# V and the gates of an mLSTM layer: from a plain product to seven products of 520-column quarters

## The chip, the cores and the metric

One core of a Trainium2 chip runs one program. Its time is device microseconds (us); the kernel before has a median of 2306.89 us over three runs (2303.06 to 2307.14). Five engines work side by side: TensorE (PE in the profile, with its weight loads apart as PEld), VectorE (DVE), ScalarE (ACT), GpSimd (POOL) and SyncE (SP), whose queue issues nearly all transfers. Each engine takes its instructions in the order in which they were written into its queue, and an instruction that waits holds up all behind it on that engine.

## The reference

A trunk of two layers over 2048 and 256 tokens of width 1024, in f32. The second layer is a bidirectional mLSTM:

```
xn = rms_norm(x, norm_g[1])
proj = xn @ w_in            # 1024 x (512 q + 512 k + 1024 v + 1024 o + 1024 z + 16 gates)
g = (g + gate_bias).reshape(B, S, 4, MLSTM_HEADS)   # input and forget gate, forward and backward
h = mlstm_chunkwise(q, k, v, ig_f, fg_f) + flipped(mlstm_chunkwise on the flipped sequence)
y = x + (norm(h) * sigmoid(o) * silu(z)) @ w_out
```

The change touches the columns v and g of `proj`: 1024 + 16 = 1040 columns for each token.

## The kernel before, in words

The 2304 tokens are 18 tiles of 128 (`NT`), worked on in nine pairs (`PAIRS`). The program runs in stages: attention (`attn_core`), then products of all tokens with a weight matrix: z (`attn_gate`), the attention's output (`attn_out`), q and k, and V with the gates (both in `mlstm_qkv`), z and o of the mLSTM in two passes (`mlstm_gates_states`), and at last `mlstm_core`. In this text the two passes of `mlstm_gates_states` are called oz0 and oz1.

To come near f32 with a faster number format, every operand is split into a high and a low part (`split` for tokens, `part` for weights: ScalarE makes the high part, VectorE the low one), and every product of a 128x128 block of tokens with a block of weights is three matmuls: high by high, high by low, low by high. Each of them is a weight load (of the tokens) and a matmul over the columns (of the weights).

All these passes but one are **Winograd passes** (`winograd_pass`). A pair of tiles (256 tokens by 1024) times 1024 columns is seen as a 2x2 by 2x2 product of blocks (a quarter of the weights is 512 rows by 512 columns) and done with seven block products in place of eight. A block product has four 128-row steps, so it is 12 matmuls of 512 columns. Weights and tokens are combined for that: `combinations` makes t1 to t4 from the four quarters on VectorE and ScalarE, and `winograd_x` makes s1 to s4 (kept in DRAM as `xsum` and read back by later passes over the same tokens, `sums=True`). Since the combinations are not ready when a pass starts, its first pair is done plainly (`plain`, eight block products, 96 matmuls), and its `between` gives the slots of b12 back and starts the combinations. `following` makes a pass load the first tokens of the next one in its last pair.

In a Winograd pair, the sums go through PSUM tiles: a and b from the pool `pj` (two banks), c and d from `cdp` (two banks). `use(t, b, o, u)` takes a finished block: o is in PSUM, u a partial sum in SBUF to be added, or None.

Weights live in **slots** (`slot`, a high and a low tile of 128x512 each): 16 in the pool w, 8 in wy, 5 in wx (`NWX`), 29 in all. Seven operands of four slots are 28; the plain first pair needs b12 besides, whose four slots come back in the middle of it.

V and the gates are the exception, the lower half of `mlstm_qkv` (lines 688 to 704). Their weights are loaded by `load_w` in units of 512, 272 and 256 columns, and each tile is done by `project` (lines 398 to 400): eight 128-row steps of three matmuls for each of the three units, so 72 matmuls a tile, with one `pj` bank a unit; `cdp` is not used in this stage. ScalarE copies the first unit out (line 698), VectorE the others with the gates (lines 700 to 703).

Then `gate_sums` makes running sums of the gates for all tokens, a long chain of small operations on VectorE with a few matmuls, and the Winograd pass oz0 starts. Within an engine, the order of instructions is made by a scheduler when the program is built: it lists what is ready by its own costs, so work of the next stage is moved into the tail of the one before.

Of the kernel before, what the change touches and what calls it, by code (L numbers as in the profile page):

```python
# [28 lines left out]
VW = DV + 2  # L29
# [8 lines left out]
NWX = 5  # L38
# [23 lines left out]
class Trunk:  # L62
# [122 lines left out]
    def part(self, raw, g=None):  # L185

        nc = self.nc
        hi, lo = self.slot()
        if g is None:
            nc.scalar.copy(hi[:], raw)  # L190
            nc.vector.tensor_sub(lo[:], raw, hi[:].bitcast(F32))  # L191
        else:
            nc.scalar.activation(hi[:], raw, AF.Copy, scale=g)
            nc.vector.scalar_tensor_tensor(lo[:], raw, g, hi[:].bitcast(F32), ALU.mult, ALU.subtract)
        return hi[:], lo[:], 512

    def quarter(self, src, c0, row, col, i):
        kt = row * 4 + i
        return self.stage(src[kt * 128:(kt + 1) * 128, c0 + col * 512:c0 + (col + 1) * 512], "raww")

    def quarters(self, src, c0, g=None):

        W = {k: [None] * 4 for k in ("b12", *WOPS)}
        for row in range(2):
            gk = lambda i: None if g is None else g[:, row * 4 + i:row * 4 + i + 1]
            for i in range(4):
                for col in range(2):
                    op = f"b{row + 1}{col + 1}"
                    W[op][i] = self.part(self.quarter(src, c0, row, col, i), gk(i))
                    self.at[op, i] = self.taken.pop()  # L210
        return W

    def combinations(self, src, c0, W, g=None):
# [9 lines left out]
        for i in range(4):  # L223
            b11, b12, b22, b21 = (self.quarter(src, c0, r, c, i) for r, c in ((0, 0), (0, 1), (1, 1), (1, 0)))
            t2 = self.raw("raww")[:, :512]
# [63 lines left out]
    def half_product(self, o, xs, ws, more=False):  # L289

        nc = self.nc
        for i, ((xh, xl), (wh, wl, _)) in enumerate(zip(xs, ws)):
# [4 lines left out]
    def winograd(self, pair, X, W, use, side):  # L297
# [3 lines left out]
        u = lambda: self.mid.tile([128, 512], F32, tag="u", name="u", bufs=3)[:]  # L301
# [25 lines left out]

    def plain_x(self, s0, s1, X):
# [5 lines left out]
    def plain(self, pair, X, W, use, between, side):  # L334
# [5 lines left out]
        def passes(k, row, i):  # L340
            (xh, xl), (wh, wl, _) = X[k[0], row][i], W[f"b{row + 1}{k[1] + 1}"][i]
# [15 lines left out]
    def winograd_pass(self, xT, src, c0, g, use, done=None, following=None, first=None, sums=False):  # L357


        self.at = {}  # L360
        W = self.quarters(src, c0, g)
        X = first
# [9 lines left out]
        for n, pair in enumerate(PAIRS):  # L372
# [6 lines left out]
            if n == 0:  # L379
                self.plain(pair, X, W, use, between, side)  # L380
            else:
                self.winograd(pair, X, W, use, side)
# [278 lines left out]
    def mlstm_qkv(self, first):  # L661
        nc, tc, a = self.nc, self.tc, self.a
        with ExitStack() as st:
# [25 lines left out]
            self.release()  # L689
            for t in range(NT):  # L690
                xs = self.load_x(self.xn2T[t])
                v = p.tile([128, MH, VW], F32, tag="v", name="v", bufs=2)
                nc.gpsimd.memset(v[:, :, DV:], 1.0)
                for b in range(3):
                    pj = self.pj()
                    self.project(pj, xs, w[b])
                    if b == 0:
                        nc.scalar.copy(v[:, 1:3, :DV], pj[:].rearrange("p (h d) -> p h d", h=2))
                    elif b == 1:
                        nc.vector.tensor_copy(v[:, 0, :DV], pj[:, :DV])  # L700
                        nc.vector.tensor_add(self.gates[:, t, :], pj[:, DV:DV + 16], self.gbias)
                    else:
                        nc.vector.tensor_copy(v[:, 3, :DV], pj[:, :DV])
                nc.sync.dma_start(self.v[t][:], v[:])
# [428 lines left out]
```

## Time and profile before

| | us |
|---|---|
| median of three runs | 2306.89 |
| the profiled execution | 2307.11 |
| its span, first to last instruction | 2305.0 |
| PE busy | 2217.8 (96%) |
| PEld busy | 1763.9 (77%) |
| DVE busy | 1505.6 (65%) |
| ACT busy | 1136.4 (49%) |
| first and last copy of V out of PSUM by ScalarE (line 698) | 1286.5 to 1486.7 |

"Busy" is the time in which an engine has at least one instruction running. Matmuls overlap: one of 512 columns shows about 0.4 us, though the next starts 0.23 us after it. So what a matmul costs is read from start to start. PEclk is the share of the TensorE clock that the chip granted. A row of windows gives, for each stretch, its length and the busy time of each engine with the number of instructions. A row of groups gives the busy time, the mean duration of one in ns, and behind the second bar the idle time of the engine before them with what ended it.

### The profile page before, as it was taken

What the parts mean: (1) busy time and instruction counts of PE and PEld (TensorE: products, weight loads), DVE (VectorE), ACT (ScalarE), POOL (GpSimd) and SP (SyncE); (2) the same over time, 40 slices, a digit from 0 to 9 for tenths busy, and PEclk for the clock granted to TensorE, in tenths of its full rate; (3) what the DMA queues carried; (4) which work ended last, traced back from release to release, by engine and by line L of the source; (5) the groups of instructions that cost most, each with busy time, mean ns of one, the idle gap of its engine ahead of it and who ended that gap; (6) DMA issues with size and microseconds to landing.
All of it is one profiled execution on the core that took longest, in us unless ns stands there. A gap on an engine that the chain in (4) does not pass through costs nothing. (4 is left out here: it accounts for less than half of the span.)

```text
span 2305.0 us, 33121 instructions
## 1 busy us (share of the span) xinstructions
PE 2217.8 (96%) x11102; PEld 1763.9 (77%) x11102; DVE 1505.6 (65%) x3303; ACT 1136.4 (49%) x2565; POOL 464.1 (20%) x392
## 2 busy tenths in 40 slices
PE   8999999999899999999999999999999977999998
PEld 7767676767567887788788899978878866888887
DVE  7565656565887779668656422386697576777784
ACT  6454545454764335557534411365464455454453
POOL 3211121211001222332000000022232243333320
PEclk9999999999999999999999999999999997999999
DMA  7111111111225447657655622356576565665641
GB/s 266 48 39 49 39 48 39 49 38 40 92 65 197 150 159 237 214 197 267 217 175 183 228 92 92 124 197 196 187 252 211 182 229 194 203 195 197 210 161 69
DMA packets 181802, 347.40 MB, mean 151 GB/s; under 512 B 20064, under 2 KB 22912, under 8 KB 181632
## 3 DMA queue, kind: packets, MB, share of 16 engines
q1 hardware_dynamic: 181488, 345.27, 45.0%
q8 instruction: 88, 1.44, 0.3%
q14 instruction: 82, 0.67, 0.1%
q10 hardware_dynamic: 144, 0.01, 0.0%
HBM read 247.93 MB, written 97.28 MB: 150 GB/s over the span
## 5 line engine op out<-in xcount | busy, mean ns | idle before, releaser
L398 PE MATMUL pj<-whi,xhi 128*128 128x512 f32 (+2 forms) x1152 | 433.6, 377 | 9.1 <-ACT whi L168 5.6
L123 ACT CAST xhi<-rawx 128x512 fp32r<-128x512 f32 x372 | 228.5, 618 | 418.4 <-PE pj L399 108.5
L400 PE MATMUL pj<-whi,xlo 128*128 128x512 f32 (+2 forms) x1152 | 423.2, 372 | 8.3 <-DVE xlo L124 8.3
L399 PE MATMUL pj<-wlo,xhi 128*128 128x512 f32 (+2 forms) x1152 | 426.3, 370 | 0.0
L124 DVE TENSOR_TENSOR xlo<-rawx,xhi 128x512 fp32r<-128x512 f32 x338 | 249.5, 743 | 106.7 <-ACT xhi L123 94.9
L400 PEld LDWEIGHTS pj<-whi,xlo 128*128 128x128 f32 x1152 | 218.0, 189 | 52.3 <-DVE xlo L124 11.4
L398 PEld LDWEIGHTS pj<-whi,xhi 128*128 128x128 f32 x1152 | 217.7, 189 | 51.3 <-issue 8.8
L399 PEld LDWEIGHTS pj<-wlo,xhi 128*128 128x128 f32 x1152 | 217.9, 189 | 36.6 <-issue 2.4
L536 ACT ACTIVATE Sm<-Sm,nm 128x384 f32<-128x384 f32 (+1 forms) x288 | 167.0, 581 | 95.0 <-DVE nm L530 88.6
L293 PE MATMUL pj<-whi,xhi 128*128 128x512 f32 x480 | 192.4, 401 | 2.7 <-DVE e L874 1.3
L294 PE MATMUL pj<-wlo,xhi 128*128 128x512 f32 x480 | 191.5, 399 | 0.4 <-DVE wlo L191 0.4
L295 PE MATMUL pj<-whi,xlo 128*128 128x512 f32 x480 | 191.3, 399 | 0.0
L525 DVE CUSTOM_DVE_ANT_0 Sm<-s,mask 128x384 f32<-128x384 f32 (+1 forms) x272 | 136.0, 530 | 72.1 <-PE s L523 69.0
L549 PE MATMUL ptp<-ident,Sm 128*128 128x128 f32 x800 | 135.3, 280 | 9.8 <-DVE PT L552 6.4
L549 PEld LDWEIGHTS ptp<-ident,Sm 128*128 128x128 f32 x800 | 94.6, 141 | 54.3 <-ACT Sm L536 19.0
L293 PE MATMUL c<-whi,xhi 128*128 128x512 f32 x320 | 127.5, 399 | 2.9 <-ACT whi L190 2.9
L293 PE MATMUL d<-whi,xhi 128*128 128x512 f32 x320 | 128.1, 400 | 1.4 <-DVE x L640 1.4
L294 PE MATMUL c<-wlo,xhi 128*128 128x512 f32 x320 | 127.1, 397 | 0.7 <-DVE wlo L191 0.7
L295 PE MATMUL c<-whi,xlo 128*128 128x512 f32 x320 | 127.0, 397 | 0.0
L294 PE MATMUL d<-wlo,xhi 128*128 128x512 f32 x320 | 126.4, 395 | 0.0
L295 PE MATMUL d<-whi,xlo 128*128 128x512 f32 x320 | 126.3, 395 | 0.0
L522 PE MATMUL s<-KH,Q 128*128 128x384 f32 (+1 forms) x288 | 106.0, 379 | 10.2 <-DVE mx L525 4.6
(242 smaller groups left out, 4650.9 us busy)
## 6 DMA issues: line engine op xcount, KB each, us to landing
rawx<-xn2T SPq DMA_DIRECT2D x128, 256.0 KB, 3.6
x<-x SPq DMA_DIRECT2D x108, 256.0 KB, 3.9
rawx<-xT SPq DMA_DIRECT2D x72, 256.0 KB, 3.0
raww<-w_oz SPq DMA_DIRECT2D x64, 256.0 KB, 4.8
rawx<-xsum SPq DMA_DIRECT2D x64, 256.0 KB, 3.0
raww<-w_qkvg SPq DMA_DIRECT2D x40, 256.0 KB, 4.3
v<-v SPq DMA_DIRECT2D x18, 516.0 KB, 3.8
rawx<-v SPq DMA_DIRECT2D x36, 258.0 KB, 2.8
```

Source lines behind the costliest of these rows:

```text
L123: nc.scalar.copy(hi[:], src)
L124: (eng or nc.vector).tensor_sub(lo[:], src, hi[:].bitcast(F32))
L293: nc.tensor.matmul(o, xh, wh, start=i == 0 and not more, stop=False, skip_group_check=more)
L294: nc.tensor.matmul(o, xh, wl, start=False, stop=False, skip_group_check=more)
L295: nc.tensor.matmul(o, xl, wh, start=False, stop=i == 3, skip_group_check=more)
L398: nc.tensor.matmul(o[:, :n], xh, wh, start=kt == 0, stop=False)
L399: nc.tensor.matmul(o[:, :n], xh, wl, start=False, stop=False)
L400: nc.tensor.matmul(o[:, :n], xl, wh, start=False, stop=kt == KT - 1)
L522: nc.tensor.matmul(S[:, :nk, :], q, KH[:, g, win, :], start=True, stop=False)
L525: nc.vector.tensor_tensor_reduce(Sm[:, :nk], S[:, :nk], mask[:, t % 3, win, :], 1.0, MASKED, ALU.add, ALU.max, mx[:, c:c + 1])
L536: nc.scalar.activation(Sg[c][:, :nk], Sg[c][:, :nk], AF.Exp, bias=nm[:, c:c + 1], scale=HD ** -0.5, accum_out=rs[:, c:c + 1])
L549: nc.tensor.transpose(tp[:, c, :], Ss[g][c][:, j, :], self.ident[:])
```

## The change

V and the gates become a Winograd pass too, over the same nine pairs. Each half of the weights is now 520 columns: 512 of V and 8 gates, so the host orders the columns as v[:, :512], g[:, :8], v[:, 512:], g[:, 8:]. 520 columns don't fit one PSUM bank, so a block lies in two pieces: 256 columns in a `pj` bank and 264 in a `cdp` bank (`CUTS`), and each matmul of a block product becomes two, with the same tokens. Two pieces are one accumulator (`wide`); the four banks make two of them, so the seven products of a pair (`winograd_wide`) share two accumulators, where a Winograd pair of 512 columns has four banks of its own. The first pair (`plain_wide`) does the right half of the columns first (b12, b22), then `between`, then the left half. `use` writes half of a V tile at a time. The pass loads the first tokens for oz0, and takes its own from the q/k pass. The weight slots become 520 columns wide and number 28 (`NWX` 4), for all passes.

```diff
-NWX = 5
+NWX = 4
+NW = 520
+CUTS = ((0, 256), (256, NW))
...
     def slot(self):
         pool, tag = self.free.popleft()
-        lo = pool.tile([128, 512], F32R, tag=tag + "l", name="wlo", bufs=1)
-        hi = pool.tile([128, 512], F32R, tag=tag + "h", name="whi", bufs=1)
+        lo = pool.tile([128, NW], F32R, tag=tag + "l", name="wlo", bufs=1)
+        hi = pool.tile([128, NW], F32R, tag=tag + "h", name="whi", bufs=1)
...
     def quarters(self, src, c0, g=None):
+        for row, i, col in [(r, i, c) for r in range(2) for i in range(4) for c in range(2)] if self.width == 512 else \
+                [(r, i, c) for c in (1, 0) for r in range(2) for i in range(4)]:
...
+    def wide_product(self, o, xs, ws, first=True, last=True):
+        nc = self.nc
+        for i, ((xh, xl), (wh, wl)) in enumerate(zip(xs, ws)):
+            for j, (x, w) in enumerate(((xh, wh), (xh, wl), (xl, wh))):
+                for p, (c0, c1) in zip(o, CUTS):
+                    nc.tensor.matmul(p, x, w[:, c0:c1], start=first and i + j == 0, stop=last and i == len(ws) - 1 and j == 2,
+                                     skip_group_check=True)
+
+    def winograd_wide(self, pair, X, W, use, side):
...
+        product = lambda o, x, w, more=False: self.wide_product(o, X[x], W[w], not more)
+        a, b = self.wide(), self.wide()
+        product(a, "a11", "b11")
+        u1, u2, u3 = u(), u(), u()
+        for y, p in zip(cut(u1), a):
+            nc.scalar.copy(y, p)
+        side()
+        product(b, "s2", "t2")
+        add(u2, u1, b)
+        side()
+        product(a, "a12", "b21", True)
+        use(t0, 0, a, None)
+        side()
+        b = self.wide()
+        product(b, "s3", "t3")
+        add(u3, u2, b)
+        side()
+        a = self.wide()
+        product(a, "s1", "t1")
+        use(t1, 1, a, cut(u3))
+        side()
+        product(b, "a22", "t4", True)
+        use(t1, 0, b, cut(u2))
+        side()
+        product(a, "s4", "b22", True)
+        use(t0, 1, a, cut(u2))
+        side()
+
+    def wide(self):
+        c = self.cdp.tile([128, 512], F32, tag="cd", name="c", bufs=2)
+        return [x[:, :c1 - c0] for x, (c0, c1) in zip((self.pj(), c), CUTS)]
+
+    def plain_wide(self, pair, X, W, use, between, side):
+        for b in (1, 0):
+            o = [self.wide() for _ in pair]
+            for row in range(2):
+                for i in range(4):
+                    for t in range(2):
+                        ws = W[f"b{row + 1}{b + 1}"]
+                        self.wide_product(o[t], X[t, row][i:i + 1], ws[i:i + 1], row + i == 0, row == 1 and i == 3)
+                    if i % 2:
+                        side()
+            for t in range(2):
+                use(pair[t], b, o[t], None)
+            if b:
+                between()
...
-            self.winograd_pass(self.xn2T, a["w_qkvg"], 0, self.g[:, 1], use, first=first, sums=True)
-            w = self.load_w(a["w_qkvg"][:, 1024:], [[512], [272, 256]], self.g[:, 1])
...
+            first = self.winograd_pass(self.xn2T, a["w_qkvg"], 0, self.g[:, 1], use, following=self.xn2T[:2], first=first, sums=True)
+            def use(t, b, o, u):
+                v = p.tile([128, 2, VW], F32, tag="v", name="v", bufs=4)
+                nc.gpsimd.memset(v[:, :, DV:], 1.0)
+                gates = self.gates[:, t, b * 8:(b + 1) * 8]
+                for h in range(2):
+                    if u is None:
+                        nc.scalar.copy(v[:, h, :DV], o[h][:, :DV])
+                    else:
+                        nc.vector.tensor_add(v[:, h, :DV], o[h][:, :DV], u[h][:, :DV])
+                nc.vector.tensor_add(gates, o[1][:, DV:], self.gbias[:, b * 8:(b + 1) * 8])
+                if u is not None:
+                    nc.vector.tensor_add(gates, gates, u[1][:, DV:])
+                nc.sync.dma_start(self.v[t][:, 2 * b:2 * b + 2], v[:])
+
+            return self.winograd_pass(self.xn2T, a["w_qkvg"], 1024, self.g[:, 1], use, following=self.xn2T[:2], first=first,
+                                      sums=True, width=NW)
```

The scheduler's order changes with it. In the changed kernel's rows the line numbers are its own: L338 is the matmul of `wide_product`, L414 to L416 are those of `plain` (342 to 344 before), L126 and L193 the high parts of tokens and weights, L767 the copy of V. A number behind a name tells one buffer from another, and in brackets stands the engine that an instruction waits for.

**TensorE in the middle of the stage.** Before, one tile's units follow each other, each in its own `pj` bank:

```order
L400 MATMUL pj_13967<-whi_13118,xlo_13962 128x512
L398 MATMUL pj_13993<-whi_13124,xhi_13955 128x272 [waits DVE_49]
L399 MATMUL pj_13993<-wlo_13123,xhi_13955 128x272
L400 MATMUL pj_13993<-whi_13124,xlo_13956 128x272
...
L398 MATMUL pj_14020<-whi_13128,xhi_13955 128x256 [waits Activation_49]
L399 MATMUL pj_14020<-wlo_13127,xhi_13955 128x256
```

Now, where the fifth product of a pair follows the fourth and the sixth the fifth:

```order
L338 MATMUL c_13944<-whi_13442,xlo_13721 128x264
L338 MATMUL pj_13979<-whi_13353,xhi_13759 128x256 [waits Activation_49]
L338 MATMUL pj_13979<-wlo_13352,xhi_13759 128x256
...
L338 MATMUL c_13978<-whi_13353,xhi_13759 128x264 [waits DVE_49]
L338 MATMUL c_13978<-wlo_13352,xhi_13759 128x264
...
L338 MATMUL c_13978<-whi_13446,xlo_13760 128x264
L338 MATMUL pj_13945<-whi_13357,xhi_13796 128x256 [waits DVE_49]
L338 MATMUL pj_13945<-wlo_13356,xhi_13796 128x256
```

Units of 512, 272 and 256 columns have become pairs of 256 and 264. A product waits for the copies of the product before the last one, out of the same accumulator.

**TensorE at the end of the stage.** Before, single matmuls of oz0's plain pair (L342 to L344, into the `cdp` banks that V left unused) stand between those of the last V tile:

```order
L400 MATMUL pj<-whi,xlo 128x272
L343 MATMUL c<-wlo,xhi 128x512
L398 MATMUL pj<-whi,xhi 128x256
...
L400 MATMUL pj<-whi,xlo 128x256
L344 MATMUL c<-whi,xlo 128x512
L342 MATMUL c<-whi,xhi 128x512
```

Now the last product of V ends before oz0 begins:

```order
L338 MATMUL c<-whi,xlo 128x264
L414 MATMUL pj<-whi,xhi 128x512
L415 MATMUL pj<-wlo,xhi 128x512
...
L415 MATMUL pj<-wlo,xhi 128x512
L414 MATMUL c<-whi,xhi 128x512
```

**ScalarE at the start of the stage.** Before, V's first copy stands among the next pass's weights (L193) and k and q of the last pair:

```order
L193 ACTIVATE whi<-raww,g 128x512
L676 ACTIVATE k<-k 128x512
L698 COPY v<-pj 128x2x256
L682 COPY yT<-tr 128x512
L193 ACTIVATE whi<-raww,g 128x512 x3
```

Now the copies out of the plain pair's blocks stand behind the high parts of V's own combined weights (L193):

```order
L126 CAST xhi_13253<-rawx_13251 128x512 [waits PE_49]
L193 CAST whi_13380<-raww_13362 128x520 [waits DVE_49]
L767 COPY v_13317<-pj_13194 128x256 [waits PE_49]
L767 COPY v_13323<-pj_13196 128x256 [waits PE_49]
L193 CAST whi_13376<-raww_13368 128x520 [waits DVE_49]
...
L193 CAST whi_13450<-raww_13428 128x520 [waits DVE_49]
L126 CAST xhi_13483<-rawx_13481 128x512 [waits DMAHW6_49,PE_49]
L767 COPY v_13571<-pj_13454 128x256 [waits PE_49]
```

The plain pair's second half (pj_13454) is copied out behind the last of these weights (whi_13450), and the next product that uses its bank comes after that copy.

More of the change, by code (lines that the diff above doesn't have):

```diff
@@ L187, in part @@
         nc = self.nc
-        hi, lo = self.slot()
+        hi, lo = (x[:, :self.width] for x in self.slot())
         if g is None:
-            nc.scalar.copy(hi[:], raw)
-            nc.vector.tensor_sub(lo[:], raw, hi[:].bitcast(F32))
-        else:
-            nc.scalar.activation(hi[:], raw, AF.Copy, scale=g)
-            nc.vector.scalar_tensor_tensor(lo[:], raw, g, hi[:].bitcast(F32), ALU.mult, ALU.subtract)
-        return hi[:], lo[:], 512
+            nc.scalar.copy(hi, raw)
+            nc.vector.tensor_sub(lo, raw, hi.bitcast(F32))
+        else:
+            nc.scalar.activation(hi, raw, AF.Copy, scale=g)
+            nc.vector.scalar_tensor_tensor(lo, raw, g, hi.bitcast(F32), ALU.mult, ALU.subtract)
+        return hi, lo
     def quarter(self, src, c0, row, col, i):
         kt = row * 4 + i
-        return self.stage(src[kt * 128:(kt + 1) * 128, c0 + col * 512:c0 + (col + 1) * 512], "raww")
+        n = self.width
+        return self.stage(src[kt * 128:(kt + 1) * 128, c0 + col * n:c0 + (col + 1) * n], "raww")
     def quarters(self, src, c0, g=None):
         W = {k: [None] * 4 for k in ("b12", *WOPS)}
[L204 to L210, printed above, removed]
+        for row, i, col in [(r, i, c) for r in range(2) for i in range(4) for c in range(2)] if self.width == 512 else \
+                [(r, i, c) for c in (1, 0) for r in range(2) for i in range(4)]:
+            gk = None if g is None else g[:, row * 4 + i:row * 4 + i + 1]
+            op = f"b{row + 1}{col + 1}"
+            W[op][i] = self.part(self.quarter(src, c0, row, col, i), gk)
+            self.at[op, i] = self.taken.pop()
         return W
@@ L300, in winograd @@
         t0, t1 = pair
-        u = lambda: self.mid.tile([128, 512], F32, tag="u", name="u", bufs=3)[:]
+        u = lambda: self.mid.tile([128, NW], F32, tag="u", name="u", bufs=3)[:, :512]
         a, b = self.pj(), self.pj()
@@ L355, in plain, with winograd_pass @@
             side()
-    def winograd_pass(self, xT, src, c0, g, use, done=None, following=None, first=None, sums=False):
-        self.at = {}
+    def winograd_pass(self, xT, src, c0, g, use, done=None, following=None, first=None, sums=False, width=512):
+        self.at, self.width = {}, width
         W = self.quarters(src, c0, g)
+        plain, winograd = (self.plain, self.winograd) if width == 512 else (self.plain_wide, self.winograd_wide)
         X = first
@@ L379, in winograd_pass @@
             if n == 0:
-                self.plain(pair, X, W, use, between, side)
+                plain(pair, X, W, use, between, side)
             else:
-                self.winograd(pair, X, W, use, side)
+                winograd(pair, X, W, use, side)
             for _ in gen:
@@ L860, in mlstm_gates_states @@
             operands(NT - 1)
-            X = None
             for b in range(2):
```

35 lines of the change are left out of this document (14 added, 21 removed).

## The prediction

> **What bounds the kernel now.** I read the page first, then the stages in windows, then single matmuls of the V stage.
>
> ```profile
> span 2305.0 us, 33121 instructions
> PE 2217.8 (96%) x11102; PEld 1763.9 (77%) x11102; DVE 1505.6 (65%) x3303; ACT 1136.4 (49%) x2565; POOL 464.1 (20%) x392
> PEclk9999999999999999999999999999999997999999
> ```
>
> TensorE is busy for 96% of the span at full clock, so it is the first suspect; but a busy matmul may overlap another, and the share is a mean over stages. The windows tell the stages apart:
>
> ```profile
> core 0: us, PE busy (x) PEld busy (x) DVE busy (x) ACT busy (x) POOL busy (x), PEclk, DMA share, GB/s
> 900.00:940.00 40.00, 38.52 (x177) 30.55 (x176) 32.95 (x58) 22.24 (x47) 10.86 (x8) 1.00 0.76 246
> 1080.00:1107.00 27.00, 27.00 (x130) 22.23 (x129) 25.00 (x44) 21.72 (x42) 3.00 (x4) 1.00 0.85 277
> 1107.00:1130.00 23.00, 18.62 (x81) 14.90 (x80) 14.88 (x29) 12.35 (x23) 0.00 (x0) 0.93 0.78 262
> 1260.00:1297.00 37.00, 37.00 (x198) 31.42 (x197) 28.28 (x51) 25.17 (x46) 0.00 (x0) 1.00 0.80 263
> 1297.00:1480.00 183.00, 183.00 (x1158) 165.87 (x1157) 36.74 (x80) 29.73 (x49) 1.70 (x16) 1.00 0.31 106
> 1480.00:1500.00 20.00, 20.00 (x114) 17.41 (x114) 16.30 (x30) 15.42 (x24) 0.00 (x0) 1.00 0.69 229
> 1522.00:1545.00 23.00, 19.92 (x78) 15.34 (x77) 18.50 (x87) 9.07 (x16) 5.70 (x4) 0.85 0.53 176
> 1714.00:1740.00 26.00, 23.50 (x109) 18.25 (x108) 24.87 (x40) 15.32 (x28) 5.29 (x3) 1.00 0.79 269
> ```
>
> In the V stage (1297 to 1480) TensorE is busy in 183.00 of 183.00 us, while VectorE works 36.74 and ScalarE 29.73: here TensorE alone sets the time, and each matmul taken away shortens the kernel by its pitch. The entry to V (1260 to 1297) has no idle time either. The starts of the other passes do: TensorE is idle for 1.48 us near 900 to 940 (attention's output), 4.38 us behind the plain pair of q and k (1107 to 1130), 3.08 us in oz0 (1522 to 1545) and 2.50 us in oz1 (1714 to 1740). There VectorE is nearly full while the plain pair runs (25.00 of 27.00 us at 1080), since the combined weights are made then.
>
> What does a matmul cost from start to start?
>
> ```profile
> 1377.52 0.40 PE L398 MATMUL pj<-whi,xhi 128*128 128x512 f32 x1
> 1383.12 0.29 PE L398 MATMUL pj<-whi,xhi 128*128 128x272 f32 x1
> 1386.09 0.28 PE L398 MATMUL pj<-whi,xhi 128*128 128x256 f32 x1
> 1388.92 0.39 PE L398 MATMUL pj<-whi,xhi 128*128 128x512 f32 x1
> 1383.25 0.19 PEld L400 LDWEIGHTS pj<-whi,xlo 128*128 128x128 f32 x1
> 1383.38 0.19 PEld L398 LDWEIGHTS pj<-whi,xhi 128*128 128x128 f32 x1
> ```
>
> The first four rows are the first matmuls of one tile's three units and of the next tile. Each unit has 24 matmuls, so the pitch is 5.60 / 24 = 0.2333 us for 512 columns, 2.97 / 24 = 0.1238 for 272 and 2.83 / 24 = 0.1179 for 256; a tile takes 11.40 us. The pitch follows the columns. The last two rows are weight loads: each lasts 0.19 us, and the next starts 0.13 us after it, so loads overlap as well and don't set the pitch.
>
> **The change part by part.** *Matmuls.* Removed are 18 tiles of 11.40 us: 205.2 us. Added are 96 matmuls of 520 columns in the plain pair (eight block products of 12) and 8 x 84 in the Winograd pairs (seven of 12): 768, each in two pieces. For 256 columns the row above gives 0.1179; for 264 no row exists, and halfway to 272 it is 0.1208. The two together are 0.2387, so 768 x 0.2387 = 183.3 us. Alternation of two banks could cost something; the upper bound I take is the 272-column pitch for both pieces, 768 x 0.2476 = 190.2 us, the lower one is the value itself. **Gain 21.9 us (15.0 at the upper bound).**
>
> *VectorE and ScalarE in the pairs.* The rows for their prices:
>
> ```profile
> L124 DVE TENSOR_TENSOR xlo<-rawx,xhi 128x512 fp32r<-128x512 f32 x338 | 249.5, 743 | 106.7 <-ACT xhi L123 94.9 <-PE pj L294 4.3 <-PE pj L295 2.4
> L1055 DVE TENSOR_TENSOR kt<-pj,cs 128x256 f32<-128x256 f32 x18 | 7.5, 419 | 0.3 <-ACT es L533 0.3
> L701 DVE TENSOR_TENSOR scr<-pj,scr x18: 163/165/166, 1293.2 to 1493.6; 128x16 f32<-128x16 f32 x18
> L123 ACT CAST xhi<-rawx 128x512 fp32r<-128x512 f32 x372 | 228.5, 618 | 418.4 <-PE pj L399 108.5 <-PE pj L294 84.6 <-PE c L294 76.5
> L830 ACT COPY C<-cu 128x258 f32<-128x258 f32 x16 | 5.7, 372 | 3.1 <-PE cu L828 2.3 <-ACT u L305 0.8
> ```
>
> A pair has seven token splits, where two tiles had four; ten VectorE additions of about 256 columns out of PSUM (two for u2, two for u3, six in `use`), and seven small ones for the gates: 7 x 0.743 + 10 x 0.419 + 7 x 0.165 = 10.5 us on VectorE, and 7 x 0.618 + 4 x 0.372 = 5.8 us on ScalarE. Both lie beside the pair's 84 x 0.2387 = 20.05 us of TensorE and cost nothing as sums. What could cost is order: with two accumulators, a product starts when the copies of the last but one are done, so each copy has one product, 12 x 0.2387 = 2.86 us, to hide in. The slowest of these chains are, behind the third product, one token cast and two copies on ScalarE (0.618 + 2 x 0.372 = 1.36 us) with the gates on VectorE behind a low part (0.618 + 0.743 + 0.165 = 1.53), and behind the fifth two additions, the gates and one low part (0.84 + 0.17 + 0.74 = 1.75). Some 1.1 us are left, and a piece of 256 columns that is free first lets TensorE begin while the other is still copied. **Cost 0**; if that cover went, every excess over 2.86 would count at up to seven borders in eight pairs. Transfers: seven token loads a pair and four stores of half the size in place of four loads and two; at 106 GB/s in the V stage against 277 in the plain stage of q and k, there is room.
>
> *The start of V.* V now starts with a plain pair, 16 combined weights and all their VectorE work, where it had a start without idle time. The trace has four such starts. By idle time plus what the lower clock takes (length times one minus PEclk) they cost 1.5 us (900 to 940), 4.4 + 0.07 x 23 = 6.0 (q and k), 3.1 + 0.15 x 23 = 6.5 (oz0) and 2.5 (oz1): 4.1 in the mean. For the lower end: V's `use` has no transposes, while in the q/k start TensorE's queue stood behind one:
>
> ```profile
> PE tr L680 <- ACT q L672: 4.4, 1, 4.4
> ```
>
> and V's sums of tokens are read back, not made. Against it, V's copies stand on ScalarE behind casts that wait for VectorE. I take **4.0**, between 0 and 6.5.
>
> *The start of oz0.* Before, V's free `cdp` banks, VectorE and ScalarE let oz0's plain pair begin inside V (the 1480 to 1500 window has 16.30 us of VectorE work, against 4 for 20 us of the stage's middle, 36.74 x 20 / 183). Now V's last pair needs these banks, its own 10.5 us of VectorE and all 28 slots up to the end, while the chain of the gates stays where it was. What was done early comes later: VectorE has some 12 us less head start, of which the plain pair's 22 us hide most. On the other side, the first tokens are now loaded ahead, and the old start was already poor with 6.5. Bounds: 3 less to 6.5 more (such a start once over). I take **+2.0**, about as much as oz0 lies above the mean of the four (2.4), since the gate chain comes on top.
>
> *Slots and other passes.* 28 slots in place of 29: a pass's combinations find 12 free slots before b12's four return, not 13; the sixteen needed are still there when the plain pair's first half is done. The first quarter of the next pass waits for b11's last matmul, with six products of about 2.8 us (12 x 0.2333) still to run in that pair. **Cost 0**, hidden by the last pair; without that cover one quarter's load and split, a few us.
>
> *Sum.* -21.9 + 4.0 + 2.0 = -15.9 us against the profiled execution: 2305.0 in the span and 2.1 around it, 2307.1. That gives **2291.2 us**; the median of the runs is 0.2 below the profiled one, so 2291.
>
> On the clock: windows with 3.08 us and more of idle time show 0.93 and 0.85, those with 2.50 and less show 1.00. The Trainium skill (TensorE: Matmul & The Clock Gate, Part 1) has the array's clock halved after an idle window of about 3.4 us, and restored after as much work; the trace agrees about there. By it, a V start with less idle time would cost only that (2.0, the mean of the two at 1.00), one with more about 6.25: 2289.2 or 2293.5.
>
> **The rivals.** *Both starts as bad as the worst* (6.5 each): -21.9 + 13.0, 2298.2 us. For it speaks that VectorE was full at all of them; against it, that V has fewer operations there than q and k.
>
> *Neither start costs more:* 2285.2. V's tail now has oz0's tokens, and the scheduler fills the plain pair; against it, no start of a pass before was free, except V's own.
>
> *Slower: ScalarE's queue at the borders.* A token cast waits until TensorE gives back the buffer of an old token part; the copies stand behind such casts.
>
> ```profile
> ACT xhi L123 <- PE pj L399: 70.4, 31, 4.2
> ```
>
> If at one border of each pair a cast waits for a product later than the copy behind it, TensorE stands for about a product: 8 x 2.86 = 22.9 us, -21.9 + 6.0 + 22.9 gives 2314. It decides from 2 us a pair. Against it: in the order of the change each cast ahead of a copy waits for the same product as the copy.
>
> *Weight loads bind.* The stage's loads go from 18 x 72 = 1296 to 1536. The Trainium skill (Perfetto Trace Analysis, Identifying the Most-Contended Engine) measures TensorE's headroom by the busy time of the weight loads, and these are full already, 165.87 of 183 us. If they had to run one after another, 1536 x 0.19 = 292 us in place of 205.2 would give 2307.1 + 87 + 6 = 2400. Against it stand the two load rows above, 0.13 apart at 0.19 each: a busy share of loads that overlap is no bound.
>
> *No change to be told:* the upper price of the pieces and both bad starts, -15.0 + 13.0, 2305. That the change doesn't do what it says is excluded by the order: 1536 pieces stand for the 1296 matmuls.
>
> **How the numbers follow.** Forecast 0.55, with its own range from 2286 to 2296; both starts bad 0.20; neither 0.12; no change 0.06; slower at the borders 0.05; loads bind 0.02. A difference under 0.2% (4.6 us) can't be told from none by a measurement of this kernel; faster is thus below 2302.3: 0.55 + 0.20 + 0.12 = 0.87, same 0.06, slower 0.07. The range from 2284 to 2302 takes in the first three cases, 0.87.
>
> **What would show it.** Right: in the middle of the new stage a pair every 20.05 us, TensorE busy throughout, pitches of 0.118 and 0.121 in turn; TensorE idle for 1 to 5 us behind the plain pair of V, and 5 to 9 us lost at oz0. Wrong: idle time at the borders of products, with the wait named as a copy or addition of V; a clock below 1.00 in the stage; pitches above 0.124; or new idle time in the passes before V, which would be the slot that is gone.

## The result and the profile after

The changed kernel takes 2267.15 us in the median of four runs (2262.48 to 2270.59), beside 2305.15 for the kernel before (four runs, 2303.06 to 2307.14). The ratio is 0.9837, with a 95% interval from 0.9819 to 0.9856: 38 us faster, where 16 were forecast. The profiled execution took 2262.48 us, 2260.7 of them in its span.

The head of the page after:

```profile
span 2260.7 us, 34007 instructions
PE 2188.9 (97%) x11342; PEld 1759.3 (78%) x11342; DVE 1555.5 (69%) x3437; ACT 1163.0 (51%) x2627; POOL 462.1 (20%) x410
PEclk9999999999999999999999999999999997999999
```

TensorE lost 28.9 us of busy time (2217.8 to 2188.9), but the span lost 44.3. The other 15.4 us were time in which TensorE stood still. The two profiled executions lie further apart than the medians: that of the kernel before (2307.11 us) is one of its slowest, that of the kernel after the fastest of its four. The windows of the kernel after, at the stages that the prediction showed (length and busy time by engine, then the clock and the transfers):

```profile
900.00:940.00 40.00, 37.62 (x169) 30.31 (x168) 34.45 (x57) 22.85 (x46) 10.75 (x11) 0.96 0.73 237
1078.00:1105.00 27.00, 27.00 (x133) 22.30 (x132) 24.87 (x43) 23.79 (x46) 2.14 (x3) 1.00 0.94 314
1105.00:1128.00 23.00, 23.00 (x108) 18.73 (x107) 17.05 (x33) 11.66 (x23) 0.00 (x0) 1.00 0.80 260
1262.00:1301.00 39.00, 38.76 (x279) 36.09 (x277) 35.18 (x59) 28.33 (x52) 0.20 (x2) 1.00 0.92 308
1301.00:1462.50 161.50, 161.50 (x1344) 161.50 (x1345) 80.66 (x208) 56.17 (x110) 3.08 (x30) 1.00 0.55 173
1462.00:1486.00 24.00, 24.00 (x110) 19.40 (x109) 18.74 (x41) 16.56 (x27) 0.00 (x0) 1.00 0.74 247
1486.00:1509.00 23.00, 19.61 (x84) 15.24 (x83) 17.90 (x56) 9.59 (x18) 7.21 (x2) 0.93 0.58 189
1684.00:1710.00 26.00, 24.51 (x118) 20.03 (x117) 23.08 (x38) 13.97 (x26) 4.95 (x3) 1.00 0.79 258
```

V's plain pair runs beside the end of the q/k pass up to 1301, and TensorE stands for 0.24 us there. In the eight Winograd pairs behind it (1301 to 1462.5) it never stands; a pair takes 20.2 us. The surprise is the third row: behind the plain pair of q and k, a stage that the change does not touch, TensorE was idle for 4.38 us before (18.62 of 23.00), and now it is not idle at all.

Where the 44.3 us went can be read from two marks on TensorE, the last matmul of the q/k pass and the last one of oz1. V begins ahead of the first mark, so its first matmul is shown too. Here they are for the kernel before, the kernel after, and the kernel before with 28 slots (the first experiment below), three rows each:

```profile
1270.81 0.39 PE L398 MATMUL pj<-whi,xhi 128*128 128x512 f32 x1
1291.09 0.39 PE L295 MATMUL d<-whi,xlo 128*128 128x512 f32 x1
1886.17 0.40 PE L295 MATMUL d<-whi,xlo 128*128 128x512 f32 x1
```

```profile
1262.16 0.28 PE L338 MATMUL pj<-whi,xhi 128*128 128x256 f32 x1
1279.09 0.39 PE L299 MATMUL d<-whi,xlo 128*128 128x512 f32 x1
1853.18 0.40 PE L299 MATMUL d<-whi,xlo 128*128 128x512 f32 x1
```

```profile
1266.42 0.39 PE L398 MATMUL pj<-whi,xhi 128*128 128x512 f32 x1
1282.72 0.39 PE L295 MATMUL d<-whi,xlo 128*128 128x512 f32 x1
1876.23 0.40 PE L295 MATMUL d<-whi,xlo 128*128 128x512 f32 x1
```

Up to the first mark, V has run 24 matmuls of 512 columns and 16 of 272 in the kernel before, 32 of 256 in the kernel after, and 24 of 512 and 10 of 272 with 28 slots. At their pitches these are 7.6, 3.8 and 6.8 us, and the table counts them to V:

| us | to the end of q/k, V's matmuls taken out | V, oz0 and oz1 | mLSTM core |
|---|---|---|---|
| before | 1283.5 | 602.7 | 418.8 |
| after | 1275.3 | 577.9 | 407.5 |
| gain | 8.2 | 24.8 | 11.3 |
| before with 28 slots | 1275.9 | 600.3 | 412.7 |

Only the middle column was in the sum of the prediction, with 15.9. Of the 44.3 us, 19.5 lie in stages that work on the same operands as before, and 13.7 of these are gained as well in the kernel with 28 slots. The kernel before has one profile alone, and the experiments show that a stage of one kernel can differ by some 4 us between two executions, so no single entry is surer than that.

### The profile page after: what moved, and what is told of

It is laid out like the page before. It is cut to its first block, busy times and chain, and to the rows that moved or that the text cites. A ratio compares the mean times of both kernels' runs of the same rounds, so it can differ in the third digit from the quotient of the medians.

```text
span 2260.7 us, 34007 instructions
## 1 busy us (share of the span) xinstructions
PE 2188.9 (97%) x11342; PEld 1759.3 (78%) x11342; DVE 1555.5 (69%) x3437; ACT 1163.0 (51%) x2627; POOL 462.1 (20%) x410
## 4 chain that ended last, share of the span: by engine, by line
PE 79%; DVE 8%; ACT 5%; DMA 4%; issue 2%; POOL 2%; SPq 0%; DVEq 0%; POOLq 0%; ACTq 0%
PE pj L471 6%; PE pj L473 6%; PE pj L472 6%; PE pj L297 4%; PE pj L299 4%; PE pj L298 4%; PE c L338 4%; PE pj L338 4%; PE ptp L622 3%; PE o L634 3%; PE c L297 3%; PE c L298 3%; PE c L299 3%; PE d L299 3%; PE d L298 3%; PE d L297 3%
## 5 line engine op out<-in xcount | busy, mean ns | idle before, releaser
L126 ACT CAST xhi<-rawx 128x512 fp32r<-128x512 f32 x396 | 243.7, 618 | 446.8 <-PE c L338 94.2
L127 DVE TENSOR_TENSOR xlo<-rawx,xhi 128x512 fp32r<-128x512 f32 x362 | 267.6, 743 | 94.7 <-ACT xhi L126 88.3
L471 PE MATMUL pj<-whi,xhi 128*128 128x512 f32 x720 | 294.5, 411 | 9.2 <-ACT whi L171 5.5
L473 PE MATMUL pj<-whi,xlo 128*128 128x512 f32 x720 | 283.7, 402 | 3.5 <-DVE xlo L127 3.5
L472 PE MATMUL pj<-wlo,xhi 128*128 128x512 f32 x720 | 285.6, 397 | 0.0
L297 PE MATMUL pj<-whi,xhi 128*128 128x512 f32 x480 | 192.2, 400 | 4.9 <-ACT whi L193 3.4
L298 PE MATMUL pj<-wlo,xhi 128*128 128x512 f32 x480 | 190.3, 397 | 0.0
L299 PE MATMUL pj<-whi,xlo 128*128 128x512 f32 x480 | 190.0, 396 | 0.0
L471 PEld LDWEIGHTS pj<-whi,xhi 128*128 128x128 f32 x720 | 136.1, 189 | 44.1 <-issue 8.8
L473 PEld LDWEIGHTS pj<-whi,xlo 128*128 128x128 f32 x720 | 136.1, 189 | 41.5 <-issue 6.5
L472 PEld LDWEIGHTS pj<-wlo,xhi 128*128 128x128 f32 x720 | 136.1, 189 | 30.4 <-issue 2.4
L622 PE MATMUL ptp<-ident,Sm 128*128 128x128 f32 x800 | 135.5, 280 | 10.5 <-DVE PT L625 7.1
```

The lines of the kernel that those rows point to most:

```text
L126: nc.scalar.copy(hi[:], src)
L127: (eng or nc.vector).tensor_sub(lo[:], src, hi[:].bitcast(F32))
L297: nc.tensor.matmul(o, xh, wh, start=i == 0 and not more, stop=False, skip_group_check=more)
L298: nc.tensor.matmul(o, xh, wl, start=False, stop=False, skip_group_check=more)
L299: nc.tensor.matmul(o, xl, wh, start=False, stop=i == 3, skip_group_check=more)
L471: nc.tensor.matmul(o[:, :n], xh, wh, start=kt == 0, stop=False)
```

## The experiments

Each of these kernels computes the whole reference. Times are medians; ratios are to the kernel before, run on the same chip beside it (2301 to 2303 us). A kernel's rows have its own line numbers.

**One part alone: 28 slots, V as before.**

```diff
-NWX = 5
+NWX = 4
```

> The kernel before with 28 weight slots of 512 columns in place of 29, nothing else. Theory 'slots': the idle time behind the plain pair of q and k (6 us with its slow clock before, none now) went because the 29th slot went and the order with it, so this kernel loses it too: 2293 to 2300 us against 2305, TensorE busy in 23 of 23 us behind that plain pair. Rival 'V': the early tokens and the V stage behind it made the difference; then this kernel stays within 2 us of 2305 and keeps some 4 us of idle time there.

2288.21 us, 0.9935 (0.9916 to 0.9954); in a second session 2286.67, 0.9938 (0.9919 to 0.9957):

> The kernel before with 28 slots once more, for a narrower interval beside the kernel above: 0.9925 to 0.9955 of the kernel before; at the lower end the gap to 29 slots with the spare last (0.9957) is real, at the upper end there is none.

So one slot less makes the kernel 14 to 15 us faster, more than the first of these runs forecast (2293 to 2300 us). As in the changed kernel, TensorE has no idle time behind the plain pair of q and k:

```profile
1105.00:1128.00 23.00, 23.00 (x106) 18.56 (x105) 16.59 (x32) 12.63 (x25) 0.00 (x0) 1.00 0.75 256
```

Three eighths of the gain belong to a line that the prediction put at nothing.

**The other part alone: V in the new pass, but all nine pairs plain.**

```diff
-            if n == 0:
+            if n == 0 or all_plain:
                 plain(pair, X, W, use, between, side)
```

with no combinations made, and the tokens of each pair loaded as in the first.

> The changed kernel with eight block products in all nine pairs of V (no combined weights, tokens loaded plainly), everything else as changed. Theory 'matmuls': the Winograd form of V is worth its matmuls alone, 8 pairs x 12 x 0.2387 = 22.9 us, so 2267 + 23 = 2290, and the rest of the gain (15 us) stays with the new arrangement. Rival 'all from the V stage': without the Winograd pairs nothing of the gain is left, 2305. If V's plain pair and oz0's start suffer from V's combined weights, this kernel is better than 2290 by what they cost.

2290.39 us, 0.9944 (0.9926 to 0.9962), 23 to 25 us slower than the change (0.9837). Seven products for eight in eight pairs were worth 22.9 by the pitches (8 x 12 x 0.2387), and what is left without them is about the slot's gain again. Within the intervals the two parts add up.

**The first tokens not loaded ahead.**

```diff
-first = self.winograd_pass(... g[:, 1], use, following=self.xn2T[:2], first=first, sums=True)
+self.winograd_pass(... g[:, 1], use, first=first, sums=True)
```

> The changed kernel without the early loads of the next pass's first tokens at V and at oz0 (each pass loads its own when it starts). Theory 'preload': the free start of V comes from tokens that are ready; then V and oz0 start with idle time of 3 to 6 us each, 2273 to 2279. Rival 'scheduler': it moves these loads ahead by itself, and the kernel stays within 2 us of 2267.

2268.44 us, 0.9843 (0.9821 to 0.9866): no difference that can be told from the change's 0.9837. In the two traces the transfers stand in the same order, and but for three instructions so does the work of every engine: the scheduler puts these loads early by itself, so the run does not show what early tokens are worth.

**V's combinations a half later**, `between` behind the whole plain pair.

```diff
-            if b:
+            if not b:
                 between()
```

> The changed kernel with V's combined weights begun after the whole plain pair, not after its first half. My sum had 4 us for V's start and 0.5 came. If that was so since VectorE has slack there (my own count of its work ends some 3 to 8 us ahead of the second Winograd product), a start 11 us later shows as 3 to 8 us: 2270 to 2275. If the combined weights bind at once, about 11: 2278. If the scheduler moves them back, 2267.

2265.34 us, 0.9839 (0.9814 to 0.9864): no difference either. Here the trace has the order of the changed kernel on every engine and for every transfer: the scheduler undid the edit, so this run is the changed kernel once more and says nothing of what later combinations would cost. The next experiments leave V and go to the slot.

**What does a 29th slot cost?** With 29 slots, a pass that holds 28 leaves one free. The queue of free slots hands that one out first, so the first weight of the next pass, here V's, is made in the middle of the plain pair. The trace of the kernel before shows it on ScalarE (start, duration, idle time before in brackets with what ended it):

```profile
1109.27 0.72 ACT L168 ACTIVATE whi<-raww,g 128x512 fp32r<-128x512 f32 x1 [2.90 <-DMA raww<-w_qkvg]
1109.90 0.71 ACT L229 ACTIVATE raww<-raww,g 128x512 f32<-128x512 f32 x1
1110.51 0.71 ACT L230 ACTIVATE raww<-raww,g 128x512 f32<-128x512 f32 x1
1111.13 0.60 ACT L190 CAST whi<-raww 128x512 fp32r<-128x512 f32 x1
1111.63 1.06 ACT L672 COPY q<-pj 128x512 f32<-128x512 f32 x2
```

V's first weight (L168) waits 2.90 us for its transfer, and q's copies (L672) stand behind it; TensorE needs them for its transposes and waits 4.4 us. With 28 slots the copies stand ahead of the same multiplications (L229 and on):

```profile
1099.36 1.06 ACT L672 COPY q<-pj 128x512 f32<-128x512 f32 x2
1101.30 0.72 ACT L229 ACTIVATE raww<-raww,g 128x512 f32<-128x512 f32 x1 [0.87 <-DVE raww L227]
```

My first theory was that the early weight costs the time. Two kernels keep 29 slots and hand the spare out last, one in all passes, one only between q/k and V:

```diff
-        self.free.extend(self.taken)
+        self.free = deque(self.taken + list(self.free))
```

```diff
         self.winograd_pass(self.xn2T, a["w_qkvg"], 0, self.g[:, 1], use, first=first, sums=True)
+            self.free.rotate(-1)
```

> The kernel before with its 29 slots, but the slots that a pass gives back are queued ahead of the one that is left over, so the spare is taken last and no weight of the next pass can be made before a slot of the last pair comes free. Theory A, the weight that the spare lets in early costs the time (its cast stands on ScalarE ahead of the copies of q and waits 2.90 us for its transfer, and it holds a staging buffer): all of what 28 slots gave goes with it, 2286 to 2291 us (-12 to -17), and the wait of 4.4 us for q's copy at the start of the q/k pass is gone. Theory B, the early weight itself costs little and the number of slots matters because with 28 the list of ScalarE's work comes out in another order (q's copies 12 places earlier, the casts of v at the core's start ahead of a third E): in this kernel the order has the second but not the first, so the core's start gains about 5 us, the q/k start at most the 2.90 us, 2294 to 2299 us. Theory C, nothing but the count matters: 2303 us, as before.

> The kernel before with 29 slots, where the spare is moved to the queue's end once, between the q/k pass and the load of V's weights, so that V's first weight no longer stands in the q/k pass's plain pair. Theory A: the q/k start's 6.1 us of idle time go to 0 to 1 and V's start stays at 0, so 2296 to 2299 us. Theory B: ScalarE's order keeps the copies of q behind four combination casts, so only the 2.90 us of the waiting cast can go, 2300 to 2303 us.

2296.85 us, 0.9972 (0.9960 to 0.9984), and 2298.02, 0.9981 (0.9971 to 0.9991). Theory A falls: the spare in last place gives 6.5 us, less than half of the slot's gain. The second time lies where theory A had forecast it (2296 to 2299), but not for its reason: the wait at the q/k start did not go. There the second kernel shows why V's weight by itself was not the cause. ScalarE there, and TensorE's wait in 1072 to 1125:

```profile
1109.06 0.72 ACT L229 ACTIVATE raww<-raww,g 128x512 f32<-128x512 f32 x1 [2.96 <-DVE raww L227]
1109.69 0.70 ACT L230 ACTIVATE raww<-raww,g 128x512 f32<-128x512 f32 x1
1110.31 0.60 ACT L190 CAST whi<-raww 128x512 fp32r<-128x512 f32 x1
1110.81 1.06 ACT L672 COPY q<-pj 128x512 f32<-128x512 f32 x2
```

```profile
PE tr L680 <- ACT q L672: 3.6, 1, 3.6
```

The early weight is gone, and the next instruction in the queue waits in its place, 2.96 us for VectorE's combination, which waits 2.43 us for a transfer of the same weights. What counts is the place of q's copies in ScalarE's list. The last q/k matmul stays at 1291.1 in that kernel; with the spare last in all passes, where the lists change from the attention's output on, it comes at 1282.8, as with 28 slots. The 4 us of the second kernel lie in later stages and aren't explained.

**The place of q's copies by itself.** The spare stays first. The combinations of q/k are written behind the uses of q, and the third and fourth may not start their multiplications on ScalarE ahead of q's second copy; in the first kernel this holds for one of the two multiplications, in the second for both.

```diff
+                with self.tc.issue_after(self.hold[1]) if self.hold and i > 1 else ExitStack():
+                    nc.scalar.mul(b11, b11, g1)
-                nc.scalar.mul(b11, b11, g1)
                 nc.scalar.mul(b12, b12, g1)
```

> The kernel before with 29 slots and its spare as it was; in the q/k pass alone the combinations are written behind the uses of q, and the multiplications by g of the third and fourth combination on ScalarE may not be issued ahead of the second copy of q, as the list of the kernel with 28 slots happens to have it. If the place of q's copies on ScalarE is what makes TensorE idle at the q/k start, the wait of 4.4 us for it falls below 1.5 us and the time by 3 to 5 us, to 0.998 to 0.9987 of the kernel before. Rival: the two combinations that are held back come late for the first Winograd product that needs them, and what is gained is lost there: no change, 0.9995 to 1.0005.

> As the run with q's copies first, 29 slots, spare as before, but both multiplications by g of the third and the fourth combination stand behind q's copies; in that run one of them (the second of the third combination) still stood ahead of them and waited 2.73 us for VectorE, which waited for a transfer. If q's copies stand in a queue behind an instruction that waits for a late transfer, the wait of TensorE for them goes from 2.6 us to below 0.5, the last q/k matmul comes at 1283 to 1285 us (1291.1 before, 1286.4 in that run) and the time is 0.9965 to 0.9975 of the kernel before. Rival: the two late combinations hold up the first Winograd products instead: 0.998 to 1.

2296.03 us, 0.9976 (0.9964 to 0.9989), and 2294.47, 0.9975 (0.9963 to 0.9987). In the first, one multiplication (L232) still stands ahead of the copies (L677 there) and waits:

```profile
1107.14 0.72 ACT L232 ACTIVATE raww<-raww,g 128x512 f32<-128x512 f32 x1 [2.73 <-DVE raww L228]
1107.77 1.05 ACT L677 COPY q<-pj 128x512 f32<-128x512 f32 x2
```

```profile
PE tr L687 <- ACT q L677: 2.6, 1, 2.6
```

In the second nothing waits ahead of them, and the window behind the plain pair is full again:

```profile
1102.40 1.07 ACT L677 COPY q<-pj 128x512 f32<-128x512 f32 x2
1103.35 0.73 ACT L231 ACTIVATE raww<-raww,g 128x512 f32<-128x512 f32 x1
```

```profile
1105.00:1128.00 23.00, 22.67 (x107) 17.91 (x106) 19.37 (x36) 14.19 (x26) 0.00 (x0) 1.00 0.81 267
```

TensorE's wait for q goes 4.4, 3.6, 2.6, 0 as the copies move from 1111.6 to 1110.8, 1107.8 and 1102.4, and the last q/k matmul of the second kernel comes at 1281.7, as with 28 slots (1282.7 and 1281.8). So the idle time at the start of the q/k pass is explained: a copy in a queue behind an instruction whose data come late. Not all of the 9.4 us up to there come from it. In these two profiles TensorE's list is the same up to the last matmul of the plain pair, which comes at 1107.49 in the kernel before and at 1104.46 in this one:

```profile
1107.49 0.40 PE L344 MATMUL c<-whi,xlo 128*128 128x512 f32 x1
```

```profile
1104.46 0.39 PE L346 MATMUL c<-whi,xlo 128*128 128x512 f32 x1
```

These 3.0 us are the spread of executions. What the order takes away is the 4.38 us of idle time and the 1.6 us of slow clock in the window of the kernel before (0.07 of 23), less the 0.33 that are idle now: 5 to 6 us, and the medians differ by 5.7. The spread shows in the core too: both kernels have the same order there on every engine, and it took 418.8 and 415.1 us.

**Both at once:** spare last and q's copies first, the first form in one kernel, the second form in another.

> 29 slots with the spare taken last, which gave 6.5 us, and q's copies ahead of the third combination's multiplications; in this kernel's list v's casts stand ahead of the third E by themselves. If early weights and ScalarE's order are the whole of what the 29th slot costs, 10 to 15 us, 0.9935 to 0.9957 of the kernel before, as with 28 slots. If q's copies add nothing once the spare is last, 0.997 as before.

> The same with the spare taken last. The last q/k matmul at 1279 to 1282 us, as with 28 slots; what stays to the 28 slots' 0.9936 is then the core's: 0.995 to 0.9965 of the kernel before. If the 28 slots gain in another way up to there, the last q/k matmul stays at 1283 to 1287.

2293.41 us, 0.9957 (0.9942 to 0.9972), and 2294.54, 0.9969 (0.9958 to 0.9981). By their medians they do not reach the 28 slots. In the second the start of q/k got worse, at least in the profiled execution (3.5 us above the median): with q's copies out of the way, a cast of tokens was late, since it waited 3.5 us for its transfer; the last q/k matmul came at 1286.5, and TensorE paid twice. Its rows, start and duration:

```profile
1124.78 0.79 PE L295 MATMUL pj<-whi,xhi 128*128 128x512 f32 x1 [3.27 <-ACT xhi L124]
1125.37 0.63 PE L296 MATMUL pj<-wlo,xhi 128*128 128x512 f32 x1
...
1128.79 0.60 PE L296 MATMUL pj<-wlo,xhi 128*128 128x512 f32 x1
1129.21 0.41 PE L297 MATMUL pj<-whi,xlo 128*128 128x512 f32 x1
1129.46 0.39 PE L295 MATMUL pj<-whi,xhi 128*128 128x512 f32 x1
```

```profile
1125.00:1129.00 4.00, 4.00 (x10) 3.13 (x11) 2.94 (x5) 0.00 (x0) 0.00 (x0) 0.50 0.87 319
```

**The core.** Its part of the slot's gain is 6 us in the profiled executions (418.8 to 412.7); up to 4 of them can be the spread that the last kernels showed. The clearest difference in the lists is on ScalarE: before, the casts of the first v (L807) stand behind the exponentials of the third tile's E; with 28 slots they stand ahead. One kernel with 29 slots imposes that order, another both orders.

```diff
+                    with tc.issue_after(self.vh1) if t == 2 and d == 0 else ExitStack():
                         for h in range(MH):
                             nc.scalar.activation(E[:, d, h], E[:, d, h], AF.Exp, bias=self.u[:, d, t, h:h + 1])
```

> The kernel before with 29 slots; the exponentials of the third tile's first E in the mLSTM core may not be issued ahead of the casts of v's parts of the first two tiles, which is the order of the lists with 28 slots. If that order makes the core shorter, TensorE's wait for v's cast falls from 11.6 us to 4 to 7 us and the time by 4 to 6 us, 0.9974 to 0.9983 of the kernel before. Rival: the wait only moves to the next operand (the second v, E's third tile, the state update), 0.999 to 1.001.

> The kernel before with 29 slots and both orders of ScalarE from the two runs above. If the two are separate causes, their gains add: 7 to 11 us, 0.995 to 0.997 of the kernel before, half to three quarters of what one slot less gave (14.5 us). If the 29th slot costs in another way than by ScalarE's order (the early weights themselves), at most 3 us, 0.9987 to 1.

2302.00 us, 0.9997 (0.9984 to 1.0010), and 2295.46, 0.9965 (0.9953 to 0.9978). The rival is right for the first: no gain. TensorE's waits in the core's first 85 us, for the kernel before and for the one with v's casts first:

```profile
PE num L948 <- ACT vh L807: 11.6, 1, 11.6
PE s L919 <- DVE E L929: 10.0, 1, 10.0
```

```profile
PE s L921 <- DVE E L932: 9.7, 1, 9.7
PE num L951 <- ACT vh L807: 6.8, 1, 6.8
PE num L953 <- POOL qs L936: 6.2, 1, 6.2
```

The wait for v's cast falls by 4.8 us, and a wait of 6.2 us for GpSimd's qs takes its place. The time of the second kernel lies where gains that add were forecast (0.995 to 0.997), but one of the two gave nothing by itself, and 0.9965 can't be told from the 0.9976 of the other. The last run has the spare last and both orders; its list on every engine came out the same as that of spare last and q's copies first, since v's casts stand ahead there anyway, so it is a second measurement of that kernel:

> 29 slots with the spare taken last, q's copies ahead of the third combination's multiplications and the casts of v ahead of the third tile's E (its list has that order with or without being told). If the gap of 4.6 us that the last run left to the 28 slots lies in the core's list, which changes with every small edit, this one lands anywhere from 2287 to 2295 us beside a kernel before of 2301 to 2303, 0.993 to 0.997; if it comes from the slots themselves (a 29th costs time wherever it stands), it stays 4 to 6 us behind the 28 slots run beside it.

2294.39 us, 0.9970 (0.9958 to 0.9981), against 0.9938 (0.9919 to 0.9957) for the 28 slots beside it. The intervals just miss each other, though that of the same kernel's first measurement (0.9942 to 0.9972) overlaps. So the gap is likely, not certain: 29 slots with a better order give 7 to 10 us, 28 slots 14 to 15. Where it lies is open. The core took 415 to 420 us in the kernels with the spare last against 411 and 413 in the two executions with 28 slots, but 414.9 and 418.5 of these belong to one and the same list. No entry of the lists was found that makes the gap.

**V's order for all passes:** in the changed kernel, every plain pair does one column half after the other. The changed kernel ran again beside it.

```diff
-        at = [(t, b) for b in range(2) for t in range(2)]
+        at = [(t, b) for b in (1, 0) for t in range(2)]
...
+        for b in (1, 0):
+            for row in range(2):
+                for i in range(4):
+                    for t in range(2):
+                        passes((t, b), row, i)
```

> The changed kernel with the order that V's plain pair has (all products of the second column half, then those of the first, the second half's quarters loaded first) in the plain pairs of all passes. In the changed kernel TensorE loses about 0.5 us at V's plain pair, against 4.2 at the attention output's, 6.4 at the first o/z pass's and 2.0 at the second's. If the order by halves is why V's loses little, these 12.6 us fall to 1 to 4 and the time to 2254 to 2260 us. Rival: the combinations need all four quarters and start only after the second column half is in, with half of the pair's time left for them, and they become late by what is gained, 2262 to 2275 us.

> The changed kernel once more, beside the three others on one chip: 2262 to 2271 us, 0.982 to 0.986 of the kernel before.

2263.18 us, 0.9824 (0.9810 to 0.9839), beside 2264.05, 0.9830 (0.9816 to 0.9845): no difference. The order by halves does not make the other starts free: with it TensorE still stands for 1.59 us at the attention's output (880 to 920), 0.69 at oz0 and 2.78 at oz1. V's pass without that order was not run, so why V's own start is cheap stays open. The second execution of the changed kernel also shows how far a single look at a start can be trusted. In this window of it, oz0's start, which stood for 3.39 us in the first execution, stands for 0.60:

```profile
1485.00:1508.00 23.00, 22.40 (x102) 17.69 (x101) 22.04 (x77) 11.51 (x21) 3.15 (x3) 1.00 0.61 198
```

## Why the prediction was wrong, step by step

**Matmuls: right.** 21.9 us were forecast. With all pairs plain the time is 23 to 25 us longer (22.9 by the pitches), and V, oz0 and oz1 together are 22.0 us shorter than with 28 slots and V as before (below). The pitch came nearly as worked out (matmuls inside one product of the kernel after):

```profile
1351.53 0.28 PE L338 MATMUL pj<-whi,xhi 128*128 128x256 f32 x1
1351.65 0.28 PE L338 MATMUL c<-whi,xhi 128*128 128x264 f32 x1
...
1352.12 0.28 PE L338 MATMUL c<-whi,xlo 128*128 128x264 f32 x1
1352.25 0.28 PE L338 MATMUL pj<-whi,xhi 128*128 128x256 f32 x1
```

Three pairs of pieces take 0.72 us (1351.53 to 1352.25), 0.240 each, beside 0.2387 worked out. So alternating between two banks costs at most 0.002 us a pair of pieces, some 1 us in all.

**VectorE and ScalarE in the pairs: right, cost 0.** Eight pairs fill 1301 to 1462.5, so VectorE works 80.66 / 8 = 10.1 us a pair (10.5 worked out) and ScalarE 7.0 (5.8), and TensorE is busy in 161.50 of 161.50 us. The rival of ScalarE's queue had its casts waiting, but TensorE did not wait for them. The waits of the kernel after from 1262 to 1462, and TensorE's alone from 1262 to 1450:

```profile
ACT xhi L126 <- PE c L338: 93.8, 47, 2.3
```

```profile
PE pj L338 <- ACT xhi L126: 0.2, 1, 0.2
```

**Start of V, 4.0 forecast: too dear.** TensorE stands for 0.24 us up to the end of V's plain pair. The value was the mean of four starts, put on V without asking what each of them waits for. The prediction quoted one such wait, 4.4 us for q's copy at the q/k start, and V has no transposes that could wait like this. In the other three it waited for other things: 1.1 us for a cast of tokens at the attention's output, 2.9 for a combined weight in oz0, and 1.3 for e and 1.1 for low parts of weights in oz1. V has such casts and weights too, and there they came in time. Why is not shown.

**Start of oz0, +2.0 forecast: not confirmed.** 3.39 us idle in one execution and 0.60 in the other, beside 3.08 before; with what the lower clock takes, 5.0 and 0.6 beside 6.5. The term is smaller than the spread of one look. Nor did the prediction's border for the clock hold, full at 2.50 us of idle time and less: in the kernel after, the window from 900 to 940 has 2.38 us of idle time and a clock of 0.96.

Together these three terms were forecast at -15.9. Counted as in the table, V, oz0 and oz1 went from 602.7 to 577.9 and 576.3 in two executions of the change, -24.8 and -26.4. Beside the 28 slots with V as before (600.3 and 597.8) it is -22.0 in the mean. So the matmuls' 21.9 arrived whole, and the 6.0 that the sum put on the two starts did not: these two terms were mis-sized.

**Slots, "cost 0, hidden by the last pair": this step failed.** It asked only whether a weight would come too late with one slot less, and looked only for a loss. It did not ask what the 29th slot was used for. With it gone, the lists of all engines change from the attention's output on, and 14 to 15 us go: 5 to 6 at the q/k start, where the order of q's copies alone gives them, and the rest in places that the runs do not tell apart. The signal that the prediction named for the slot, new idle time in the passes before V, came with the opposite sign: there was less. Worse, the wait that the slot's gain ends at the q/k start was quoted, 4.4 us for q's copy, and only used as a reason for V's price; its releaser on ScalarE was not followed one step further, to the weight and the multiplications ahead of the copy, whose data came late. With nothing for the two starts and 14 to 15 us for the slot, the same sum gives -36 to -37, beside 38 measured.

Of the rivals, "neither start costs more" (2285.2) was nearest, and 18 us off, which is the slot and a few us more. No rival had a gain in stages that the change leaves alone. The loads, which were to bind at 2400, are busy for 161.50 of 161.50 us, and the pitch still follows the columns.

## What to carry to other kernels

When a change frees or removes a buffer, ask what the spare one let in early, and where those instructions stand in the queues of engines that hand data to the bound engine: earlier work of the next stage can hold up a copy that this stage needs. When a scheduler writes the order, any change of size or buffers rewrites the lists elsewhere; measure such a line by itself before its gain or loss is put to the rest of the change. Before an edit that made no difference is read as an answer, see whether the order on the engines changed at all; for two of these runs it hardly did or did not. And follow every quoted wait one step back, to what its releaser stood behind.

## What the runs showed that was not expected

Weight loads busy for 161.50 of 161.50 us cost nothing: they overlap each other, and TensorE's time still followed the columns. After TensorE had been idle for some 3.3 us (3.27 by the row above), matmuls of 512 columns ran at 0.43 us from start to start in place of 0.23, until 4.4 us later, with a granted clock of 0.50; this wait cost about 2 us more than it lasted. And the start of one pass can differ by 4 us, slow clock included (oz0, 5.0 and 0.6), between two executions of one kernel that agree within 1 us in total (spans 2260.7 and 2261.6), so a term of 2 us for one start can't be read from one profile.
